# Decay factors from running sums of g by transposes and a DVE pass; the 16 columns for beta and steps ride on a chunk of v

## Chip, core and metric

One core of a Trainium2 chip runs the whole program; the metric is the device time of one execution in microseconds. PE is the matmul engine, DVE the vector engine, ACT the scalar engine, POOL the fourth compute engine, SP the engine that only issues transfers. Each engine takes its instructions in order and stops at the first one whose inputs, or whose output buffer, are not ready.

## The reference

Two blocks over 256 tokens of 1024 channels, all in fp32. The first block holds two attention layers and two feed-forward layers. The second, the "hybrid layer", projects the normed input by one wide matrix `w_in` and feeds two branches. The change touches the gated delta rule (8 heads) and the first head of the retention (4 heads):

```python
proj = xn @ w_in
qa, ka, va, za, beta_logit, a_dt, qb, kb, vb, gb, gate_a, gate_b = _split_cols(proj, IN_SIZES)
...
beta = jax.nn.sigmoid(beta_logit)
g = -jnp.exp(a_log) * jax.nn.softplus(a_dt + dt_bias)
oa = chunk_gated_delta_rule(qa, ka, va, beta, g)
...
g_cum = jnp.cumsum(g, axis=-1)
decay = jnp.exp(jnp.where(causal, g_cum[..., :, None] - g_cum[..., None, :], -jnp.inf))
...
lower = jnp.where(strict, jnp.einsum('bhncd,bhnmd->bhncm', k_beta, k) * decay, 0.0)
attn = jnp.where(causal, jnp.einsum('bhncd,bhnmd->bhncm', q, k) * decay, 0.0)
```

`beta_logit` and `a_dt` are 8 columns each of `w_in`, the 16 columns of the title; `vb` has 512 columns for each retention head. The kernel works with the delta rule over all 256 tokens as two tiles of 128, so a head's decay factors are three 128 x 128 blocks: tile 0 with itself, tile 1 with tile 0, tile 1 with itself.

## The kernel before

Every product with a weight is done as three: an fp32 operand is held as a high part and a low part, and hi x hi, hi x lo and lo x hi are summed in PSUM. Weights are streamed in pieces: a transfer brings `raw`, ACT writes the high part `hi` (line 188), DVE writes the low part `lo = raw - hi` (line 197, in passes of at most 512 columns), and PE multiplies (helper `mm`, line 134). One `hi`/`lo` half is 1024 columns; four halves and four `raw` buffers are in flight. Activations are split likewise: `OH`/`OL` hold the input of the second block before its norm's factors are known, `XH`/`XL` the normed one (`renorm`, lines 519 to 525). Transposes are fp32 matmuls against the identity (helper `tr`, line 145; it is also what turns a column of per-token factors into a row, as for `RT`).

A chunk is a run of products that ends in PSUM and has a post function that takes it out. The chunk kinds that matter here: `X_pair` (512 columns, tokens on the partitions, 8 pieces, two banks of 128x512), `X_chunk` (256 columns, 4 pieces, one bank), `N_chunk` (16 columns, columns on the partitions, 24 matmuls in one piece) and `W_pair` (two chunks of 256 columns at once, 8 pieces, two banks). Side work (norms, splits, attention, the decays) is written as Python generators; each call of `others()` after a piece runs every active generator to its next `yield`, and `pause(n)` lets n pieces pass. So the order of each engine's instructions is fixed when the program is built. PSUM has two banks of each of the tags `w` and a few of `s` and `d`; a tag's banks are taken in turn.

At the turn from the first block to the second the order is: the last feed-forward (`ffn(1, resid2)`); its residual `resid2`, which completes x by pairs of channel tiles, writes `REG` = x times a gain, splits it into `OH` and `OL` (ACT line 680, DVE line 691) and adds up the squares for two norms (`nacc` and `y`, lines 485 and 487); `X_pair(wvbp)`, which multiplies `OH`/`OL` by v of retention head 0, tile after tile as `resid2` delivers them, with the norms' sums over channels as small matmuls after its sixth piece; the factor `RT` by POOL (line 907) and its rows `RB`, `CR` (ACT lines 912 and 913); `N_chunk(wbda)` with the 16 columns; `W_pair(wqva)` for q, k and v of delta head 0; `W_chunk(wza)`, z of head 0; `wqka`, `wva` and so on for the next heads.

`decay_task` (line 937) starts from the 16 x 256 result of `N_chunk`: copied to SBUF, transposed to a token per partition, scaled by the norm's factor, then exp, log and a few passes over 16 columns make `BETA`, `NBETA` and `GG` (g, 8 heads by 2 tiles). For each head it spreads g over a 128 x 256 tile (two DVE passes, line 979), and six matmuls against constant triangles build sum differences and the mask in PSUM; ACT's Exp takes the 128 x 384 from PSUM to `DEC` (line 995). `DEC` lies in `REG`. The kernels of the delta rule (lines 1040 on) read it: `nLT` and `AT` at line 1076, with `DD` behind, line 1082.

Of the kernel before, what the change touches and what calls it, by code (L numbers as in the profile page):

```python
# [30 lines left out]
# steps that side work lets pass before it needs what others make for it  # L31
# [34 lines left out]
def body(ctx: ExitStack, tc: tile.TileContext, a):  # L66
# [17 lines left out]
    def PT(tag="side"):  # L84
        if tag == "side":
            # held within a step only: the bank taken longest ago
            age = {t: taken[t][-BANKS[t]] if len(taken[t]) >= BANKS[t] else 0 for t in "sd"}
            tag = "s" if side["dbusy"] or deferred or age["s"] <= age["d"] else "d"
        side["n"] += 1
        taken[tag].append(side["n"])  # L90
        return ps.tile([128, 512], F32, name="ps_" + tag, tag=tag, bufs=BANKS[tag])

# [16 lines left out]
    # the gains first, then x; what is needed later comes behind the first weights  # L109
# [45 lines left out]
    class Chunk:  # L155
        def __init__(self, src, cols, npieces, mm, pre=None, post=None):
# [3 lines left out]
            # pieces that come at once  # L160
# [47 lines left out]
    def ahead(i):  # L208
        """what may be loaded and split once the products of piece i are issued"""
# [50 lines left out]
    # tiles that are held over steps: no more of them than the ring has  # L260
# [17 lines left out]
    def wbank(more=0):  # L278
        """two banks in turn; two more while the norm's factors are on their way"""
        if len(deferred) >= 4:  # L280
            drain(cur["stat"])
            late(1)
        wn[0] += 1
        if len(deferred) + more >= 2 and wn[0] % 4 in (3, 0):
            return PT("d")
        return PT("w")

    wn = [0]
# [23 lines left out]
    def products(todo, xl_last=False):  # L312
        """(out, hi, lo, xh, xl, first, last): what was split last comes last"""
# [33 lines left out]
    def N_chunk(src, xs, n, post):  # L347
        """n < 128 columns in a piece"""
        def m(ck, s, hi, lo):
            xh, xl = xs  # L350
            ck.bank = PT("d")
            o = ck.bank[:n, :T]
            for k in range(8):
                c = slice(k * n, k * n + n)
                mm(o, hi[:, c], xh[:, k], k == 0, False)
                mm(o, hi[:, c], xl[:, k], False, False)
                mm(o, lo[:, c], xh[:, k], False, k == 7)
        return add(Chunk(src, 8 * n, 1, m, None, {0: lambda ck: wpost(post)(ck.bank)}))
# [4 lines left out]
    def D_chunk(grp, src, c, n, ops, post=None, pre=None, done=None):  # L363
        def m(ck, s, hi, lo):
            if c == 0:
                if s == 0:
                    grp.banks = [None] * 4
                    side["dbusy"] = True
# [21 lines left out]
    def D_tail(grp, src, n, ops, post, pre=None):  # L390
        """the last two chunks, a bank after the other"""
# [18 lines left out]
    def W_pair(src, xs, posts):  # L410
        """two chunks of outputs at once, over the tiles of x"""
# [23 lines left out]
    def X_pair(src, xs, posts):  # L435
        """512 columns, a bank for each half of the tokens"""
# [29 lines left out]
    def split(src, hi, lo):  # L466
        """the second part a step after the first"""
# [25 lines left out]
    def sum_ch(out, parts):  # L493
        """sums over the channels, a token per partition; 32 tokens at a time, as the weights' load is what they take"""
# [19 lines left out]
    def renorm():  # L514
        """the splits of x * g * r, for the chunks after the first"""
# [73 lines left out]
    # over the keys of two blocks, for the queries of the second: all of the first, or with the window  # L589
# [4 lines left out]
    # key > query: column > partition  # L594
# [16 lines left out]
    def attend(q, k, v, slot, window=False, sink=None, delay=0, done=False):  # L611
        """q, k: [128, T], a head on each half of the partitions; v(t, half) -> [128, 64]"""
# [38 lines left out]
        for h in range(2):  # L651
# [3 lines left out]
            # blocks: (q0, k0), (q1, k0), (q1, k1)  # L655
# [11 lines left out]
    # ================= the first block =================  # L667
# [7 lines left out]
    def feed_x(b, g, xs, norm, norm2=None, g2=None, first=False):  # L675
        """after xT's pair b is complete: x * g and its splits, the squares"""
# [31 lines left out]
    # attention of layer 0  # L708
# [59 lines left out]
    def tables():  # L768
        """of the second block"""
# [9 lines left out]
    # feed-forward with a short convolution  # L779
# [63 lines left out]
    # attention of layer 1  # L843
# [45 lines left out]
    # ================= between the blocks =================  # L889
# [7 lines left out]
    def stat2():  # L897
# [4 lines left out]
        # r1 = 1 / sqrt(mean x^2 + eps), and r1 r2 with r2 the factor of x g r1  # L902
# [23 lines left out]
    # ================= the second block =================  # L926
# [10 lines left out]
    def decay_task(bank):  # L937
        # beta and g, a token per partition
        b16 = TW([128, T], "e")
        cp("V", b16[:16], bank[:16, :T])  # L940
        yield
        p = PT("s")
        for t in range(2):
            PE.transpose(p[:, t * 16:t * 16 + 16], b16[:16, t * 128:t * 128 + 128], ident[:16, :16])
        bd = TW([128, 2, 16], "bd", 1)
        for t in range(2):
            V.tensor_scalar(bd[:, t], p[:, t * 16:t * 16 + 16], RTM[:, t:t + 1], None, op0=OP.mult)
# [3 lines left out]
        S.activation(e1, bd[:, :, 0:8], AF.Exp, scale=-1.0)  # L951
        S.activation(ea, P_("a_log"), AF.Exp)
        z = bd[:, :, 8:16]
# [20 lines left out]
        V.tensor_scalar(maskB, C_("gt"), -1e30, None, op0=OP.mult)  # L974

        def spread(h):
            gx = TW([128, 2, 128], "e")
            for t in range(2):
                V.tensor_scalar(gx[:, t], C_("le"), GG[:, t, h:h + 1], None, op0=OP.mult)
            return gx  # L980
        nx = spread(0)
        yield from pause(3)
        for h in range(8):
            gx = nx
            if h < 8 - 1:
                nx = spread(h + 1)
            yield
            p = PT()
            mm(p[:, 0:128], C_("gt"), gx[:, 0], True, False)
            mm(p[:, 0:128], identb, maskB, False, True)  # L990
            mm(p[:, 128:256], C_("gt"), GG[:, 0, h:h + 1].to_broadcast([128, 128]), True, False)
            mm(p[:, 128:256], ONES128, gx[:, 1], False, True)
            mm(p[:, 256:384], C_("gt"), gx[:, 1], True, False)
            mm(p[:, 256:384], identb, maskB, False, True)
            S.activation(DEC[:, h], p[:, :384], AF.Exp)
# [3 lines left out]
    def bda_post(bank):  # L999
        cur["dec"] = start(decay_task(bank))  # L1000

    def conv4(src, u, y, base):
        """src, u, y: [128, 2, T]; tiles base[i] of conv_a"""
# [37 lines left out]
    # the small blocks on the diagonal, and the transposes of the inverses  # L1041
# [4 lines left out]
    def delta_task(h, bank):  # L1046
# [6 lines left out]
        # the norms of k go into beta and v, those of q into the norm behind  # L1053
        tk, bk, nbk = (TW([128, 2], n, 1) for n in ("tk", "bk", "nbk"))
        qe, kv = (TW([128, 2], n, 3) for n in ("qe", "kv"))
        # the inverse, block by block of twice the size: D (0) and its transpose (1)
# [152 lines left out]
    def vb0_post(t):  # L1209
        def f(bank):  # L1210
            for c in range(2):
                if t == 0:
                    vbt[0, c] = hold([128, 2, 256], "v")
                cp("S", vbt[0, c][:, t], bank[:, c * 256:c * 256 + 256], RTM[:, t:t + 1])
        return f
# [554 lines left out]
```

## Time and profile before

| what | value |
|---|---|
| runs of the kernel | 1344.65, 1344.09, 1341.1 us |
| median | 1344.09 us |
| span of the profiled execution | 1341.2 us |
| that execution's own time | not recorded apart from its span; the median is 2.9 us above it |
| PE, DVE, ACT busy | 98%, 73%, 55% of the span |
| POOL busy | 2% |
| DMA | 215.79 MB, mean 161 GB/s |

The span is what the hardware profiler saw between the first and the last instruction of the one execution it recorded; the three runs are timed from outside. PE's share is that of matmuls whose ends are modelled. Times in the rows below are microseconds from the start of the span. In a row of the timeline the first number is the start, the second the duration of the group, `x4` the count of instructions in it, and `[0.31 <-DVE DD L1083]` an idle time before it with what ended it.

### The profile page before, as it was taken

Reading aid. Unit: us, or ns where it says so; the run is one execution under the profiler, and the core shown is the slowest. Engines: PE = TensorE matmul, PEld = TensorE weight load, DVE = VectorE, ACT = ScalarE, POOL = GpSimd, SP = SyncE. Lnnn points to the kernel's source line nnn. Section 1 sums busy time; section 2 is a strip of 40 time slices with the busy share of each in tenths; the row PEclk is TensorE's granted clock in tenths of the full one; section 3 lists DMA queues with packets and bytes.
Section 4 is the critical chain, followed back from the end, with each engine's and each line's share of the span. In section 5 each row is a group of like instructions: output and inputs, shape, how many; then the busy total and the mean of one; then the engine's idle time right before and its main releaser. Section 6 shows DMA issues by size and latency. Waiting matters only on the chain.

```text
span 1341.2 us, 29103 instructions
## 1 busy us (share of the span) xinstructions
PE 1317.4 (98%) x11824; PEld 1250.3 (93%) x11824; DVE 984.4 (73%) x2225; ACT 731.6 (55%) x1202; POOL 27.2 (2%) x38
## 2 busy tenths in 40 slices
PE   7999999999999999999999999999999999999998
PEld 6999999998889999999888888999999999999996
DVE  6997887778878877788778888666557556855554
ACT  6665765555765655566545544444343445655553
POOL 0000000000000000000000000000000000000000
PEclk9999999998999999999999999999999999999999
DMA  7435565554334655544333333445455564465652
GB/s 240 156 127 183 175 205 188 186 181 142 107 117 156 215 189 189 185 133 158 115 107 114 110 126 104 134 157 191 150 179 168 173 196 153 160 219 184 189 183 89
DMA packets 60470, 215.79 MB, mean 161 GB/s; under 512 B 6832, under 2 KB 7600, under 8 KB 60336
## 3 DMA queue, kind: packets, MB, share of 16 engines
q1 hardware_dynamic: 59328, 212.31, 49.1%
q8 instruction: 93, 1.52, 0.5%
q10 hardware_dynamic: 1008, 1.63, 0.4%
q14 instruction: 41, 0.34, 0.1%
HBM read 212.86 MB, written 1.05 MB: 159 GB/s over the span
## 4 chain that ended last, share of the span: by engine, by line
PE 92%; DVE 4%; ACT 2%; issue 1%; DMA 1%; POOL 0%; SPq 0%; POOLq 0%; DVEq 0%; ACTq 0%
PE ps_w L134 54%; PE ps_d L134 33%; PE ps_s L134 4%; PE ps_s L145 1%; ACT h L634 1%; DVE lo L197 1%; PE ps_d L145 1%; DMA xT<-in_x 0%; DMA raw<-in_wv0p 0%; DVE y L794 0%; ACT hi L188 0%; DVE XL L464 0%; DVE h L626 0%; DVE y L1369 0%; DVE DD L1082 0%
## 5 line engine op out<-in xcount | busy, mean ns | idle before, releaser
L197 DVE TENSOR_TENSOR lo<-raw,hi 128x512 fp32r<-128x512 f32 x801 | 519.7, 684 | 93.5 <-ACT hi L188 92.7
L188 ACT ACTIVATE hi<-raw 128x1024 fp32r<-128x1024 f32 (+1 forms) x403 | 418.1, 1046 | 168.9 <-PE ps_w L134 85.7
L134 PE MATMUL ps_w<-XH,hi 128*128 128x256 f32 x976 | 168.3, 295 | 2.5 <-ACT XH L1454 1.4
L134 PE MATMUL ps_w<-XL,hi 128*128 128x256 f32 x976 | 156.3, 283 | 0.0
L134 PE MATMUL ps_w<-XH,lo 128*128 128x256 f32 x976 | 156.1, 282 | 0.0
L134 PE MATMUL ps_w<-OH,hi 128*128 128x256 f32 x896 | 144.8, 284 | 0.0
L134 PE MATMUL ps_w<-OH,lo 128*128 128x256 f32 x896 | 142.9, 282 | 0.3 <-DVE lo L197 0.3
L134 PE MATMUL ps_w<-OL,hi 128*128 128x256 f32 x896 | 142.5, 281 | 0.0
L134 PEld LDWEIGHTS ps_w<-XH,hi 128*128 128x128 f32 x976 | 134.4, 191 | 7.8 <-ACT XH L1454 1.7
L134 PEld LDWEIGHTS ps_w<-XL,hi 128*128 128x128 f32 x976 | 133.8, 190 | 0.0
L134 PEld LDWEIGHTS ps_w<-XH,lo 128*128 128x128 f32 x976 | 133.6, 190 | 0.0
L134 PE MATMUL ps_d<-OH,hi 128*128 128x256 f32 x776 | 126.0, 283 | 0.0
L134 PEld LDWEIGHTS ps_w<-OH,hi 128*128 128x128 f32 x896 | 121.5, 188 | 3.6 <-issue 3.5
L134 PE MATMUL ps_d<-OL,hi 128*128 128x256 f32 x776 | 124.4, 281 | 0.0
L134 PE MATMUL ps_d<-OH,lo 128*128 128x256 f32 x776 | 124.3, 281 | 0.0
L134 PEld LDWEIGHTS ps_w<-OH,lo 128*128 128x128 f32 x896 | 122.1, 189 | 0.5 <-DVE lo L197 0.5
L134 PEld LDWEIGHTS ps_w<-OL,hi 128*128 128x128 f32 x896 | 121.7, 188 | 0.0
L134 PEld LDWEIGHTS ps_d<-OH,hi 128*128 128x128 f32 x776 | 104.9, 188 | 1.9 <-issue 1.7
L134 PEld LDWEIGHTS ps_d<-OL,hi 128*128 128x128 f32 x776 | 105.1, 187 | 0.3 <-DVE OL L470 0.2
L134 PEld LDWEIGHTS ps_d<-OH,lo 128*128 128x128 f32 x776 | 105.1, 188 | 0.2
L790 ACT ACTIVATE y<-u,prm 128x256 f32<-128x256 f32 x88 | 48.0, 595 | 62.4 <-DVE u L764 62.4
L764 DVE TENSOR_TENSOR u<-ps_w,RB 128x512 f32<-128x512 f32 x44 | 30.1, 689 | 63.0 <-PE ps_w L134 56.8
(378 smaller groups left out, 1644.7 us busy)
## 6 DMA issues: line engine op xcount, KB each, us to landing
raw<-in_wu SPq DMA_DIRECT2D x108, 512.0 KB, 4.2
raw<-in_wd SPq DMA_DIRECT2D x68, 512.0 KB, 3.9
raw<-in_wgb SPq DMA_DIRECT2D x24, 512.0 KB, 3.7
raw<-in_wqk SPq DMA_DIRECT2D x16, 512.0 KB, 4.0
raw<-in_wza SPq DMA_DIRECT2D x16, 512.0 KB, 3.8
raw<-in_wqkb SPq DMA_DIRECT2D x16, 512.0 KB, 4.1
raw<-in_wbra SPq DMA_DIRECT2D x16, 512.0 KB, 4.2
raw<-in_wbrb SPq DMA_DIRECT2D x16, 512.0 KB, 4.7
```

What stands on the lines that cost most here:

```text
L134: PE.matmul(out, lhsT, rhs, start=start, stop=stop, skip_group_check=True)
L145: PE.transpose(out, in_, ident)
L188: S.activation(hi[:, :w], raws[n][:, :w], AF.Copy)
L197: V.tensor_tensor(lo[:, c], raws[n][:, c], hi[:, c].bitcast(F32), op=OP.subtract)
L634: S.activation(e[h][:, c], e[h][:, c], AF.Exp, bias=nm[:, i:i + 1], accum_out=sums[:, i:i + 1])
L764: V.tensor_tensor(u, v2(bank), bc(RB, 2), op=OP.mult)
L790: S.activation(y[:, i], u[:, i], AF.Identity, bias=P_(cb, t), scale=P_(cw, 3 * t + 2))
```

## The change

The chunks at the turn are cut differently: `XN_chunk` multiplies 16 + 256 columns (the 16 for beta and the steps, and the first 256 of v of retention head 0) in one pass with tokens on the partitions, from four halves of 544 columns, and `X_chunk` does the other 256 columns; `X_pair` and `N_chunk` are gone. `vbd_post` scales the 16 columns from PSUM into `BD`, so that `decay_task` needs no copy and no transposes of its own, and starts it after tile 1. In `decay_task` three small matmuls make the running sums of g for all heads at once (`CUM`). For each head two transposes of a broadcast column of `CUM` put the sums along the free axis in PSUM; two DVE passes subtract the head's own column and take the minimum with a mask tile (0 or -1e30); ACT's Exp then works in place in `DEC`. `wbank` and `D_chunk` differ in when the sums' wait is drained and in which banks are taken. The comments of the file are gone as well; line numbers move by 4 and more.

```diff
-        if len(deferred) >= 4:
+        if len(deferred) + more >= 6:
             drain(cur["stat"])
-            late(1)
-        wn[0] += 1
-        if len(deferred) + more >= 2 and wn[0] % 4 in (3, 0):
-            return PT("d")
-        return PT("w")
-    wn = [0]
+            late()
+        return PT("w" if len(deferred) + more < 2 else "d")
...
-    def N_chunk(src, xs, n, post):
-        """n < 128 columns in a piece"""
+    def XN_chunk(src, xs, n, post):
+        w = 256 + n
         def m(ck, s, hi, lo):
             xh, xl = xs
-            ck.bank = PT("d")
-            o = ck.bank[:n, :T]
-            for k in range(8):
-                c = slice(k * n, k * n + n)
-                mm(o, hi[:, c], xh[:, k], k == 0, False)
-                mm(o, hi[:, c], xl[:, k], False, False)
-                mm(o, lo[:, c], xh[:, k], False, k == 7)
-        return add(Chunk(src, 8 * n, 1, m, None, {0: lambda ck: wpost(post)(ck.bank)}))
+            if s == 0:
+                ck.bank = [wbank(), wbank(1)]
+            todo = []
+            for kk in range(2):
+                k = 2 * s + kk
+                for t in range(2):
+                    tt = slice(t * 128, t * 128 + 128)
+                    c = slice(kk * w, kk * w + w)
+                    todo.append((ck.bank[t][:, :w], xh[:, k, tt], xl[:, k, tt], hi[:, c], lo[:, c], k == 0, k == 7))
+            products(todo, True)
+        ck = add(Chunk(src, 8 * w, 4, m, None, {3: lambda ck: [wpost(post(t))(ck.bank[t]) for t in range(2)]}))
+        ck.g = 1
...
+                    if deferred:
+                        drain(cur["stat"])
+                        late()
...
-    def decay_task(bank):
-        # beta and g, a token per partition
-        b16 = TW([128, T], "e")
-        cp("V", b16[:16], bank[:16, :T])
-        yield
-        p = PT("s")
-        for t in range(2):
-            PE.transpose(p[:, t * 16:t * 16 + 16], b16[:16, t * 128:t * 128 + 128], ident[:16, :16])
-        bd = TW([128, 2, 16], "bd", 1)
-        for t in range(2):
-            V.tensor_scalar(bd[:, t], p[:, t * 16:t * 16 + 16], RTM[:, t:t + 1], None, op0=OP.mult)
+    BD = T1([128, 2, 16], name="BD")
+    def decay_task():
+        yield from pause(1)
         e1, ea = TW([128, 2, 8], "e1", 1), TW([128, 8], "ea", 1)
         ax = TW([128, 2, 8], "axx", 1)
         sp = TW([128, 2, 8], "sp", 1)
-        S.activation(e1, bd[:, :, 0:8], AF.Exp, scale=-1.0)
+        S.activation(e1, BD[:, :, 0:8], AF.Exp, scale=-1.0)
         S.activation(ea, P_("a_log"), AF.Exp)
-        z = bd[:, :, 8:16]
+        z = BD[:, :, 8:16]
...
-        V.tensor_scalar(maskB, C_("gt"), -1e30, None, op0=OP.mult)
-        def spread(h):
-            gx = TW([128, 2, 128], "e")
-            for t in range(2):
-                V.tensor_scalar(gx[:, t], C_("le"), GG[:, t, h:h + 1], None, op0=OP.mult)
-            return gx
-        nx = spread(0)
-        yield from pause(3)
+        V.tensor_scalar(MW[:, 0:128], C_("gt"), -1e30, None, op0=OP.mult)
+        V.memset(MW[:, 128:256], 0.0)
+        yield from pause(2)
+        p = PT()
+        mm(p[:, 0:8], C_("le"), GG[:, 0], True, True)
+        mm(p[:, 8:16], C_("le"), GG[:, 1], True, False)
+        mm(p[:, 8:16], ONES128, GG[:, 0], False, True)
+        CUM = TW([128, 2, 8], "cum", 1)
+        V.tensor_copy(CUM.rearrange("p t h -> p (t h)"), p[:, 0:16])
+        yield from pause(1)
         for h in range(8):
-            gx = nx
-            if h < 8 - 1:
-                nx = spread(h + 1)
             yield
             p = PT()
-            mm(p[:, 0:128], C_("gt"), gx[:, 0], True, False)
-            mm(p[:, 0:128], identb, maskB, False, True)
-            mm(p[:, 128:256], C_("gt"), GG[:, 0, h:h + 1].to_broadcast([128, 128]), True, False)
-            mm(p[:, 128:256], ONES128, gx[:, 1], False, True)
-            mm(p[:, 256:384], C_("gt"), gx[:, 1], True, False)
-            mm(p[:, 256:384], identb, maskB, False, True)
-            S.activation(DEC[:, h], p[:, :384], AF.Exp)
+            for t in range(2):
+                tr(p[:, t * 128:t * 128 + 128], CUM[:, t, h:h + 1].to_broadcast([128, 128]))
+            V.scalar_tensor_tensor(DEC[:, h, 0:256], p[:, 0:256], CUM[:, 0, h:h + 1], MW, op0=OP.subtract, op1=OP.min)
+            V.scalar_tensor_tensor(DEC[:, h, 256:384], p[:, 128:256], CUM[:, 1, h:h + 1], maskB, op0=OP.subtract, op1=OP.min)
+            S.activation(DEC[:, h], DEC[:, h], AF.Exp)
...
-    def bda_post(bank):
-        cur["dec"] = start(decay_task(bank))
...
-    def vb0_post(t):
+    def vbd_post(t):
         def f(bank):
-            for c in range(2):
-                if t == 0:
-                    vbt[0, c] = hold([128, 2, 256], "v")
-                cp("S", vbt[0, c][:, t], bank[:, c * 256:c * 256 + 256], RTM[:, t:t + 1])
+            if t == 0:
+                vbt[0, 0] = hold([128, 2, 256], "v")
+            V.tensor_scalar(BD[:, t], bank[:, 0:16], RTM[:, t:t + 1], None, op0=OP.mult)
+            if t == 1:
+                cur["dec"] = start(decay_task())
+            cp("S", vbt[0, 0][:, t], bank[:, 16:272], RTM[:, t:t + 1])
         return f
+    def vb0_post(bank):
+        vbt[0, 1] = hold([128, 2, 256], "v")
+        for t in range(2):
+            cp("S", vbt[0, 1][:, t], bank[:, t * T:t * T + T], RTM[:, t:t + 1])
 
     for h in range(8):
         if h == 0:
-            X_pair(a["wvbp"], xsR, [vb0_post(t) for t in range(2)])
-            N_chunk(a["wbda"][0], xsR, 16, bda_post)
+            XN_chunk(a["wvbd"], xsR, 16, vbd_post)
+            X_chunk(a["wvb"][0], xsR, vb0_post)
             W_pair(a["wqva"], xsR, [qka_post(0), va_post(0)])
```

The order of the instructions at three places. First DVE where `resid2` takes out its last pair of channel tiles, whose `OL` the chunk of v waits for (before; `nacc`, `y` are the two norms' sums):

```order
L197 TENSOR_TENSOR lo<-raw,hi 128x512
L691 TENSOR_TENSOR OL<-REG,OH 128x512
L485 TENSOR_TENSOR nacc<-nacc,sq 128x512
L487 TENSOR_TENSOR nacc<-nacc 128x256
L485 TENSOR_TENSOR y<-y,sq 128x512
L487 TENSOR_TENSOR y<-y 128x256
L197 TENSOR_TENSOR lo<-raw,hi 128x512 x2
L691 TENSOR_TENSOR OL<-REG,OH 128x512
L197 TENSOR_TENSOR lo<-raw,hi 128x512
```

The same place now, with the lines moved by 4:

```order
L197 TENSOR_TENSOR lo<-raw,hi 128x512
L695 TENSOR_TENSOR OL<-REG,OH 128x512
L489 TENSOR_TENSOR nacc<-nacc,sq 128x512
L491 TENSOR_TENSOR nacc<-nacc 128x256
L489 TENSOR_TENSOR y<-y,sq 128x512
L491 TENSOR_TENSOR y<-y 128x256
L197 TENSOR_TENSOR lo<-raw,hi 128x32
L197 TENSOR_TENSOR lo<-raw,hi 128x512
L197 TENSOR_TENSOR lo<-raw,hi 128x32
L695 TENSOR_TENSOR OL<-REG,OH 128x512
L197 TENSOR_TENSOR lo<-raw,hi 128x512 x6
```

The weights' `lo` now comes in passes of 512 and 32 columns, and the last `OL` pass stands behind three of them. Its reader on PE was the seventh piece of eight of `X_pair`, behind the norms' sums; it is now the last of the four pieces of `XN_chunk`, ahead of them.

Second ACT, from the norm's rows `RB`, `CR` to the logarithm of the decays (`XH` is the renormed input; before):

```order
L912 COPY RB<-ps_s 128x256
L913 COPY CR<-ps_s 128x256
L138 ACTIVATE v<-ps_w,RT_97 128x256 x4
L525 ACTIVATE XH<-qn 128x512
L188 ACTIVATE hi<-raw 128x1024
L525 ACTIVATE XH<-qn 128x512
L188 ACTIVATE hi<-raw 128x1024
L525 ACTIVATE XH<-qn 128x512
L951 ACT_TABLE_LOAD
L951 ACTIVATE e_7960<-bd 128x16
L952 ACTIVATE ea<-prm 128x8
L956 ACTIVATE axx<-axx 128x16
```

And now:

```order
L916 COPY RB<-ps_s 128x256
L917 COPY CR<-ps_s 128x256
L138 ACTIVATE v<-ps_w,RT_97 128x256 x2
L138 ACTIVATE v<-ps_d,RT_97 128x256 x2
L529 ACTIVATE XH<-qn 128x512
L188 ACTIVATE hi<-raw 128x1024
L529 ACTIVATE XH<-qn 128x512
L949 ACT_TABLE_LOAD
L949 ACTIVATE e_7983<-BD 128x16
L950 ACTIVATE ea<-prm 128x8
L954 ACTIVATE axx<-axx 128x16
L529 ACTIVATE XH<-qn 128x512
```

The `v` passes come from two chunks, two from `ps_w` and two from `ps_d`, and are still behind `RB` and `CR`; the third `XH` pass stands between the exponentials and the second table load instead of ahead of the first.

Third PE, towards the end of `W_pair` (before; the six matmuls of head 0's decays are its last rows, those of `e`, `MW` and `GG`):

```order
L134 MATMUL ps_w<-OH,hi 128x256 x4
L134 MATMUL ps_w<-OL,hi 128x256 x4
L134 MATMUL ps_w<-OH,lo 128x256 x4
L134 MATMUL ps_w<-OH,hi 128x256 x4
L134 MATMUL ps_w<-OL,hi 128x256 x4
L134 MATMUL ps_w<-OH,lo 128x256 x4
L134 MATMUL ps_d<-e,cst 128x128
L134 LDWEIGHTS identb
L134 MATMUL ps_d<-MW,identb 128x128
L134 MATMUL ps_d<-GG,cst 128x128
L134 MATMUL ps_d<-e,ones 128x128
L134 MATMUL ps_d<-e,cst 128x128
```

And now, from the fifth piece of `W_pair` to the transposes of head 0:

```order
L134 MATMUL ps_w<-OH,hi 128x256 x4
L134 MATMUL ps_w<-OL,hi 128x256 x4
L134 MATMUL ps_w<-OH,lo 128x256 x4
L134 MATMUL ps_d<-GG,cst 128x8 x2
L134 MATMUL ps_d<-GG,ones 128x8
L134 MATMUL ps_w<-OH,hi 128x256 x4
L134 MATMUL ps_w<-OL,hi 128x256 x4
L134 MATMUL ps_w<-OH,lo 128x256 x4
L134 MATMUL ps_w<-OH,hi 128x256 x4
L134 MATMUL ps_w<-OL,hi 128x256 x4
L134 MATMUL ps_w<-OH,lo 128x256 x4
L145 MATMUL ps_d<-cst,cum 128x128 x2
```

The three 128x8 matmuls of the running sums are new and wait for `GG`; head 0's six matmuls have become two transposes of `cum`. Ahead of this stretch, `W_pair` now follows the row transposes at once, where the 24 matmuls of `N_chunk` stood between, and the two 128x16 transposes of line 944 behind its second piece are gone.

## Rows read from the trace of the kernel before

**Rows 1.** The page of before: engines; then the chain that ended last:

```profile
PE 1317.4 (98%) x11824; PEld 1250.3 (93%) x11824; DVE 984.4 (73%) x2225; ACT 731.6 (55%) x1202; POOL 27.2 (2%) x38
PE 92%; DVE 4%; ACT 2%; issue 1%; DMA 1%; POOL 0%; SPq 0%; POOLq 0%; DVEq 0%; ACTq 0%
```

**Rows 2.** The timeline of PE, from X_pair to W_pair (start, duration, what):

```profile
592.15 0.63 PE L134 MATMUL ps_w<-hi,OH 128*128 128x512 f32 x2
...
600.08 0.63 PE L134 MATMUL ps_w<-lo,OH 128*128 128x512 f32 x2
...
602.84 0.63 PE L134 MATMUL ps_w<-hi,OL 128*128 128x512 f32 x2
...
605.17 0.60 PE L145 MATMUL ps_s<-cst,RT 128*128 128x128 f32 x4
605.53 0.36 PE L134 MATMUL ps_d<-OH,hi 128*16 128x256 f32 x1
...
608.42 0.40 PE L134 MATMUL ps_w<-OH,hi 128*128 128x256 f32 x2
```

**Rows 3.** The timeline of PE, the decays, to the delta rule's DD:

```profile
611.36 0.29 PE L944 MATMUL ps_s<-cst,e 16*128 16x16 f32 x2
...
631.47 0.38 PE L134 MATMUL ps_d<-e,cst 128*128 128x128 f32 x2
...
634.72 0.72 PE L134 MATMUL ps_w<-XH,hi 128*128 128x256 f32 x4
...
645.92 0.35 PE L134 MATMUL ps_d<-DD,nLT 32*32 32x32 f32 x16 [0.31 <-DVE DD L1083]
```

**Rows 4.** The timeline of PE, a pair of fp32 128x128 transposes in retention:

```profile
702.15 0.38 PE L145 MATMUL ps_s<-cst,rt 128*128 128x128 f32 x2
702.37 0.60 PE L134 MATMUL ps_d<-AT,REG 128*128 128x256 f32 x2
```

**Rows 5.** The timeline of DVE, the end of resid2:

```profile
600.63 0.69 DVE L197 TENSOR_TENSOR lo<-raw,hi 128x512 fp32r<-128x512 f32 x1 [0.92 <-ACT hi L188]
601.24 0.68 DVE L691 TENSOR_TENSOR OL<-REG,OH 128x512 fp32r<-128x512 f32 x1
```

**Rows 6.** The timeline of ACT, the same stretch, to the passes of v:

```profile
599.55 2.19 ACT L188 ACTIVATE hi<-raw 128x1024 fp32r<-128x1024 f32 x3
...
605.81 0.37 ACT L912 COPY RB<-ps_s 128x256 f32<-128x256 f32 x1 [1.44 <-PE ps_s L145]
...
606.34 1.58 ACT L138 ACTIVATE v<-ps_w,RT 128x256 f32<-128x256 f32 x4
```

**Rows 7.** The timeline of ACT, then DVE: the chain to GG:

```profile
612.00 1.28 ACT L951 ACT_TABLE_LOAD   x1
613.30 0.22 ACT L951 ACTIVATE e<-bd 128x16 f32<-128x16 f32 x1
...
616.62 0.18 DVE L973 TENSOR_SCALAR GG<-sp 128x16 f32<-128x16 f32 x1
```

**Rows 8.** Groups of DVE instructions by line and shape:

```profile
L979 DVE TENSOR_SCALAR e<-cst,GG 128x128 f32<-128x128 f32 x16 | 3.8, 279 | 1.3 <-PE ps_s L134 1.3
L1076 DVE SCALAR_TENSOR_TENSOR nLT<-ps_d,nbk,REG 128x256 f32<-128x256 f32 x6 | 2.9, 478 | 0.0
```

**Rows 9.** The timeline of ACT, the tail of the decays and the first squares:

```profile
634.94 0.49 ACT L995 ACTIVATE REG<-ps_d 128x384 f32<-128x384 f32 x1 [0.62 <-PE ps_d L134]
...
641.88 0.42 ACT L1052 ACTIVATE sq<-qk 128x256 f32<-128x256 f32 x1
```

**Rows 10.** Timeline rows of PE behind two waits; two stretches, with PEclk, the granted clock:

```profile
325.27 0.43 PE L145 MATMUL ps_s<-cst,RTOK 128*128 128x128 f32 x2 [2.29 <-POOL RTOK L538]
326.00:333.00 7.00, 5.93 (x30) 5.67 (x29) 6.51 (x14) 2.02 (x3) 0.00 (x0) 0.53 0.42 134
1152.42 0.56 PE L134 MATMUL ps_w<-XH,hi 128*128 128x256 f32 x1 [1.42 <-ACT XH L1454]
1152.00:1157.00 5.00, 4.58 (x25) 4.58 (x26) 4.90 (x10) 2.05 (x4) 0.00 (x0) 0.66 0.00 0
```

More of the change, by code (lines that the diff above doesn't have):

```diff
@@ L1349, in body @@
         for c in range(2 if h else 0):
-            X_chunk(a["wvb"][2 * h + c - 2], xs0, vb_post(h, c))
+            X_chunk(a["wvb"][2 * h + c - 1], xs0, vb_post(h, c))
         if h > 0 and da[0] < 8:
@@ L1623, in wc @@
     def wc(w, cols):
-        return w[:, cols].reshape(8, 128, len(cols)).transpose(1, 0, 2).reshape(128, -1)
+        return np.ascontiguousarray(w[:, cols].reshape(8, 128, len(cols)).transpose(1, 0, 2).reshape(128, -1))
     def wset(w, collist):
@@ L1675, in pack @@
     gb2 = ga0 + 1024
-    out["wbda"] = wset(w, [b0 + r(16)])
+    out["wvbd"] = wc(w, np.concatenate([b0 + r(16), vb0 + r(256)]))
     qka = [np.concatenate([q0 + 128 * h + r(128), k0 + 128 * h + r(128)]) for h in range(8)]
@@ L1683, in pack @@
     out["wqkb"] = wset(w, [o + 256 * h + r(256) for h in range(4) for o in (qb0, kb0)])
-    out["wvbp"] = pair(w, vb0 + r(512))
-    out["wvb"] = wset(w, [vb0 + 256 * c + r(256) for c in range(2, 8)])
+    out["wvb"] = wset(w, [vb0 + 256 * c + r(256) for c in range(1, 8)])
     out["wgb"] = wset(w, [gb0 + 256 * c + r(256) for c in range(8)])
```

## The prediction

> **What bounds the kernel now.** I read the page first: PE is busy 98% of the span and 92% of the chain that ended last [rows 1], so time is won only where PE has less to do, and lost where PE is made to wait. PE's own timeline then shows a stretch, from X_pair to the first heads of the delta rule, with hardly an idle time in it [rows 2, 3]. So every microsecond of PE work that goes there counts, unless a wait that this work used to cover comes up. The timelines of DVE and ACT say where such covers are.
>
> Times are set against the profiled span of 1341.2 us. The median of the three runs is 1344.09, 2.9 more, and I add the change in the span to the median. About 0.3%, 4 us, is what a measurement of this kernel can tell from no change: under 1340.1 is faster, over 1348.1 slower.
>
> **PE work removed and added.** X_pair's matmuls of 512 columns start 0.233 us apart (34 of them between 592.15 and 600.08), so its 48 cost 11.2. The N_chunk's 24 take 605.53 to 608.42, 2.9, or 0.12 for 256 columns [rows 2]. Between these two, a matmul of 272 columns is 0.1275. Now 48 of 272 and 48 of 256 columns cost 6.1 + 5.8 = 11.9 against 14.1: **-2.2**. The sums over channels cost 1.8 (600.55 to 602.84, less a pair of 0.47) and stay.
>
> The two 16-row transposes go: **-0.3** by their row. Three heads of the decays took 631.47 to 634.72, so 1.08 for one and 8.7 for eight [rows 3]. Two transposes for a head take 0.22 in retention [rows 4], between other matmuls like here; with a little for breaking the stream I take 0.28, eight are 2.2. The lower end is 0.2, the upper the 1.08 of the old head, which would leave no gain. The three matmuls with 8 columns need weights of 128x128 each; nearest are the old fp32 matmuls of a head at about 0.2, so 0.7, between 0.1 and 1.1. Together 8.7 - 2.2 - 0.7: **-5.8**. PE work falls by 8.3 us in all.
>
> **Waits that come instead.** Five places.
>
> (1) *OL at the last piece of XN_chunk.* DVE writes the last OL from 601.24 on, behind a wait of 0.92 for ACT's hi [rows 5]; ACT's three hi passes there begin at 599.55, behind the squares of the norms [rows 6]. Before, PE read this OL at 602.84, after the sums [rows 2], and did not wait. Now it is read in the second product of XN_chunk's fourth piece, which PE would reach at 592.15 + 40 x 0.1275 = 597.3. The new hi passes are half as long and two lo passes shrink from 512 to 32 columns, so the OL pass ends at about 600.7 (600.1 if all of that helps, 601.9 if none). The eight matmuls that are left end at 601.7 and not at 598.3: **+3.4**. The norm's row transposes, at 605.17 before, come at 601.7 + 5.8 + 1.8 = about 609.3. I call this place R.
>
> (2) *Banks for W_pair.* It now follows the rows directly, and its two ps_w banks are held by XN_chunk until ACT has taken v out, behind RB and CR. The first v pass starts 1.17 after R [rows 2, 6], and two of them, half of the four's 1.58, end at about R + 1.9, where PE stands at R + 0.4. N_chunk's 2.9 us covered this: **+1.4**.
>
> (3) *GG for the running sums.* The sums stand behind W_pair's fifth piece: R + 1.9 + 60 x 0.12 = R + 9.1. GG was written at 616.62, R + 11.45 [rows 2, 7], by a chain that table loads of 1.28, DVE passes and its place behind renorm's passes make long. The transposes at its head go, but the log now stands behind one more XH, so I leave R + 11.3: **+2.3**. The ends are 0 (the chain moves up by the 0.6 us that the small transposes and their copy took, and by some queueing) and +3.3.
>
> A page differs here: the Trainium skill, "ScalarE: Activation LUTs", section "What ACT_TABLE_LOAD costs", counts 1.28 us for the load and about 1.38 for a drain, 2.66 in all. By it each load would hold the next activation another 1.4 us. The trace's load at 612.00 lasts 1.28, and the activation behind it started at 613.30, 0.02 after its end [rows 7], so the measurement decides and the sum stays.
>
> (4) *Bank and ACT at the end of the decays.* DVE has more to do for a head: a pass of 128x256 from PSUM is 0.48 and one of half the size at least the 0.28 of an old spread, together 0.76 or more against 0.56 for the two spreads [rows 8]. Heads 5 to 7 come in one place, and head 7 takes the bank of head 4, which DVE has to read first, behind passes of the convolution, about four heads' passes of 0.76 less the 1.4 in which PE does one piece: **+1.6**, between 0 and 3. Exp then ends late, and with it the passes that make q and k: **+0.5** at the first products of the delta rule.
>
> (5) *The first squares.* From the last head's Exp to the end of sq, which PE's next sums read, ACT's passes took 634.94 to 642.30, 7.4 [rows 9], and the change leaves them alone, while it makes PE's last three heads shorter by 0.8 each. So PE gets there early by up to 2.4, of which a part is already in (4): **+1.6**, between 0 and 2.4. The old wait of 0.31 for DD [rows 3] goes: **-0.3**.
>
> The sum: -8.3 + 3.4 + 1.4 + 2.3 + 1.6 + 0.5 + 1.6 - 0.3 = **+2.2**, and 1344.09 + 2.2 = **1346.3**; with the profile's own span, 1343.4. The saved matmuls are eaten up by chains on ACT and DVE that do not become shorter.
>
> **Rivals.**
>
> *B, PE's clock falls.* At 325.27 PE had waited 2.29 us, and the granted clock in 326 to 333 is 0.53 on average; at 1152.42 it had waited 1.42 and had 0.66 over 5 us, on its way to the lower of its two levels, 1.2 instead of 2.4 GHz, and back [rows 10]. So a fall costs 0.34 x 5 = 1.7 to 0.47 x 7 = 3.3 us. The wait for GG of 2.3 is as long as the one that fell, and is followed by three tiny matmuls; the stop at OL is the second candidate. This gives 1346.3 + 1.7 to 3.3 = 1348.0 to 1349.6, and with two falls of the larger price up to 1352.9: slower than before. It decides from a single wait of about 1.4 us on, the shorter of the two that fell. Against it: the waits may be split by pieces in between. The Trainium skill, "TensorE: Matmul & The Clock Gate", "Part 4: PE-mode transpose", says that transposes do not count as busy the same way; by that the places with six transposes in a row would be a third candidate, where 631.47 to 634.72 was full of matmuls before. No row here shows a fall at transposes: the pair at 702 is too short for it.
>
> *C, the chains follow PE.* If DVE and ACT are free enough to bring OL, v and GG sooner, the waits do not come, and PE's saving stands: 1344.09 - 8.3 = 1335.8; with (1) alone left 1339.2. For it speaks that DVE is busy only 73% and ACT 55% of the span [rows 1]; against it that OL is bound by data that resid2 delivers just then, and DVE ran from one pass to the next there.
>
> *D, the transposes cost as much as the old matmuls*, so that the change does not do what it is for on PE: PE's work falls by 2.2 + 0.3 - 0.7 = 1.8 only, and (1) to (3) stay, while (4) and (5) go because PE is later: -1.8 + 7.1 - 0.3 = +5.0, 1349.1. The pair at 702 speaks against it [rows 4], and I give it little.
>
> **Numbers.** My forecast, waits that eat the gain with no fall of the clock: 0.45, at 1346.3. B with D (0.31 and 0.05): 0.36, at 1348.0 to 1352.9. C and halves of it: 0.19, from 1335.8 to 1340. A part of the forecast's cases falls outside its band on either side in equal measure. So faster 0.19, same 0.45, slower 0.36. The range leaves out C in full and the two falls of B, and holds what the ends of the waits make of the forecast: 1337.5 to 1351.
>
> **What would show it.** In the profile after: PE's row of XN_chunk's fourth piece has a wait for DVE OL of 2 to 4 us, and the chunk ends near 601.7; the row transposes stand near 609.3, and W_pair's first matmul has a wait for ACT v of about 1.4; the 128x8 matmuls wait for DVE GG; two transposes of a head take under 0.3. DD of head 0 comes at about 648.1 where it was 645.92. PEclk under 1 between 600 and 626 would show B. If these rows have waits under 0.5 us and DD comes before 640, C holds and my forecast is wrong. If DD comes on time but the total moves, the cause lies elsewhere in the file, in banks of later chunks, and I have missed it.

## The result and the profile after

The changed kernel took 1361.13 us (median of 4 runs, 1358.97 to 1362.6), the kernel before 1343.87 beside it; the ratio is 1.013, 95% interval 1.0115 to 1.0145. The forecast was 1346.3 and the range ended at 1351: wrong, and on the slow side.

The timeline of PE of the changed kernel at the places that the prediction named (start, duration, what, wait before it):

```profile
597.78 0.67 PE L134 MATMUL ps_w<-hi,OH 128*128 128x272 f32 x4
...
604.01 0.52 PE L134 MATMUL ps_w<-lo,OH 128*128 128x272 f32 x2 [1.21 <-DVE lo L197]
605.00 0.77 PE L134 MATMUL ps_w<-hi,OH 128*128 128x272 f32 x4 [0.47 <-ACT hi L188]
606.43 1.13 PE L134 MATMUL ps_w<-hi,OL 128*128 128x272 f32 x4 [0.66 <-DVE OL L695]
...
616.56 0.60 PE L145 MATMUL ps_s<-cst,RT 128*128 128x128 f32 x4
618.27 0.87 PE L134 MATMUL ps_w<-OH,hi 128*128 128x256 f32 x4 [1.11 <-ACT v L138]
...
627.89 0.61 PE L134 MATMUL ps_d<-GG,cst 128*128 128x8 f32 x4 [2.04 <-DVE GG L971]
...
642.80 0.40 PE L145 MATMUL ps_d<-cst,cum 128*128 128x128 f32 x2 [2.40 <-DVE REG L991]
...
656.08 0.35 PE L134 MATMUL ps_d<-DD,nLT 32*32 32x32 f32 x16
```

All the waits are there. But XN_chunk, the first changed work, starts at 597.78, where X_pair started at 592.15 [rows 2]: 5.6 us were lost before any changed instruction. DD of head 0 comes 10.2 late (645.92 before [rows 3]), so the changed place adds 4.5, and the rest of the program, the same again, takes 1357.1 - 656.08 = 701.0 where it took 695.3: 5.7 more. 5.6 + 4.5 + 5.7 is the 15.9 by which the span grew.

So two thirds of the loss lie where nothing was changed. (The 5.6 and the 5.7 are not the pace alone: the granted clock also fell at other places, in before at the two of [rows 10], worth up to 3.3 and 1.7, and in the changed kernel in 15 to 20, where it was 0.66, worth up to 1.7.) PE's matmuls start further apart there. The timeline of PE of the changed kernel in the feed-forward layers of the first block, groups of four matmuls of 256 columns, three groups apart:

```profile
460.03 0.64 PE L134 MATMUL ps_d<-OL,hi 128*128 128x256 f32 x4
...
461.47 0.64 PE L134 MATMUL ps_d<-OL,hi 128*128 128x256 f32 x4
```

The same stretch of the kernel before:

```profile
460.09 0.63 PE L134 MATMUL ps_d<-OH,hi 128*128 128x256 f32 x4
...
461.51 0.64 PE L134 MATMUL ps_w<-OH,hi 128*128 128x256 f32 x4
```

Three groups take 1.44 us now and 1.42 before, 0.480 against 0.473 for one, with the granted clock at its full level in both. Some 7,850 matmuls of the program have a weight as the stationary operand and stand next to another of that kind; 1.6 ns more for each is 12.6 us. What the change does to them is not an instruction: `BD = T1(...)` is a new tile of 128 bytes per partition, allocated ahead of `raw`, `hi` and `lo`. By the memory map of the compiled programs, all hi and lo buffers start 160 bytes past a multiple of 256 before, and 32 past one after; XH, XL, OH and OL stay at 128. The sizes of the tiles in the source between OL and these buffers, each rounded up to 32 bytes, add up to the same distances: 32 past a multiple of 256 before, 160 after.

### The profile page after: what moved, and what is told of

Same layout as the page of the kernel before. It is cut to its first block, busy times and chain, and to the rows that moved or that the text cites. A ratio compares the mean times of both kernels' runs of the same rounds, so it can differ in the third digit from the quotient of the medians.

```text
span 1357.1 us, 29039 instructions
## 1 busy us (share of the span) xinstructions
PE 1322.5 (97%) x11788; PEld 1256.8 (93%) x11788; DVE 987.0 (73%) x2229; ACT 731.9 (54%) x1203; POOL 27.6 (2%) x38
## 4 chain that ended last, share of the span: by engine, by line
PE 89%; DVE 6%; ACT 3%; issue 1%; DMA 0%; POOL 0%; SPq 0%; POOLq 0%; DVEq 0%; ACTq 0%
PE ps_w L134 51%; PE ps_d L134 32%; PE ps_s L134 4%; DVE lo L197 1%; PE ps_s L145 1%; PE ps_d L145 1%; ACT hi L188 1%; ACT h L638 1%; DMA xT<-in_x 0%; DVE h L630 0%; DVE OL L695 0%; DVE y L798 0%; DVE REG L142 0%; DVE XL L468 0%; DVE nacc L489 0%
## 5 line engine op out<-in xcount | busy, mean ns | idle before, releaser
L188 ACT ACTIVATE hi<-raw 128x1024 fp32r<-128x1024 f32 (+2 forms) x404 | 418.2, 1044 | 174.5 <-PE ps_w L134 82.9
```

Of the source, the lines that this page charges most:

```text
L188: S.activation(hi[:, :w], raws[n][:, :w], AF.Copy)
```

## The experiments

**The place of the buffers by itself.** Theory L: the place sets the pace. Rival S: the pace belongs to the changed instructions, or to the chip. First the place without the change:

```diff
     GG = T1([128, 2, 8], name="GG")
+    T1([128, 32], name="PAD")
```

> The kernel before with an unused tile of 128 bytes per partition where the change puts BD, so that the weights' raw, hi and lo buffers, and all that lies behind, move by 128 bytes as they do in the changed kernel; no instruction differs. Theory L (the place of the weights' buffers sets the matmuls' pace): groups of four 256-column matmuls start 0.48 us apart instead of 0.473, and the time is 1344 + about 11 to 13 = 1355 to 1357. Rival S (the slower pace belongs to the changed instructions, or to the chip that ran them): the pace stays 0.473 and the time 1344.

Measured: 1356.03, ratio 1.0097 (1.008 to 1.0115) to the kernel before. The timeline of PE, four groups apart:

```profile
459.78 0.64 PE L134 MATMUL ps_w<-OH,lo 128*128 128x256 f32 x4
...
461.71 0.64 PE L134 MATMUL ps_d<-OH,hi 128*128 128x256 f32 x4
```

1.93 for four, 0.48 each. L holds: an unused tile costs 12.8 us. Then the change without the place:

```diff
-    BD = T1([128, 2, 16], name="BD")
...
             if t == 0:
+                bdt["x"] = TW([128, 2, 16], "bd", 1)
```

> The changed kernel with BD taken from the working pool when it is first written, behind the weights' buffers, so that raw, hi and lo lie where they lay before. Theory L: pace 0.473 again and a time of about 1361 - 12 = 1349, which is the 4 us that the waits and clock falls at the changed place cost. Rival S: 1361.

Measured: 1350.09, ratio 1.0054 (1.0035 to 1.0073). The place is worth 11 us of the 17.3. The change's own work costs 6.7 against 1343.4, the kernel before over all its runs, and 6.9 against the 1343.24 measured beside this run. The timeline of PE of this run:

```profile
592.50 0.66 PE L134 MATMUL ps_w<-hi,OH 128*128 128x272 f32 x4
...
612.00 0.60 PE L145 MATMUL ps_s<-cst,RT 128*128 128x128 f32 x4
...
623.33 1.02 PE L134 MATMUL ps_d<-GG,cst 128*128 128x8 f32 x4 [2.13 <-DVE GG L972]
...
641.28 0.40 PE L145 MATMUL ps_d<-cst,cum 128*128 128x128 f32 x2 [2.46 <-DVE REG L992]
...
654.55 0.35 PE L134 MATMUL ps_d<-DD,nLT 32*32 32x32 f32 x16
```

XN_chunk starts at 592.50, 0.35 from before's X_pair, and the rest behind DD takes 1349.5 - 654.55 = 695.0, as before. So all that is lost, is lost between them: 8.3 us. Its windows (span of the window, busy times of PE, PEld, DVE, ACT, POOL, then the granted clock, DMA share and GB/s):

```profile
595.00:605.00 10.00, 7.80 (x39) 6.83 (x38) 8.46 (x16) 6.77 (x10) 0.00 (x0) 0.72 0.56 179
605.00:610.00 5.00, 5.00 (x120) 4.85 (x119) 0.76 (x4) 1.06 (x2) 0.30 (x1) 0.87 0.80 263
...
620.00:630.00 10.00, 7.87 (x42) 7.67 (x41) 5.13 (x19) 5.31 (x6) 0.00 (x0) 0.67 0.33 107
...
640.00:650.00 10.00, 8.26 (x66) 8.04 (x67) 9.32 (x22) 7.64 (x12) 0.00 (x0) 1.00 0.41 129
```

The clock fell behind the stops at OL and lo, and again behind the wait for GG: 0.28 x 10 + 0.13 x 5 + 0.33 x 10 = up to 6.8 us of the 8.3. That is rival B, twice.

**Which places are fast.** Four places at once:

```diff
-        hi = TW([128, 1024], "hi", LA + 1, F32R)
+        hi = TW([128, 1032], "hi", LA + 1, F32R)
...
-            parts[n].append(TW([128, 1024], "lo", LA + 1, F32R))
+            parts[n].append(TW([128, 1032], "lo", LA + 1, F32R))
```

> The kernel before with each hi and lo buffer 32 bytes longer, so that the four hi buffers start at 160, 192, 224 and 0 and the four lo buffers at 32, 64, 96 and 128 bytes past a multiple of 256 (before: all at 160; changed: all at 32). Theory L: the pace of the matmuls differs from one hi buffer to the next in turn, with lo at 32 the slow one (0.120 each) and hi at 160 the old one (0.1183); whether another place is faster still is what the run is to show. Rival S: one pace for all.

Measured: 1336.0 (one run). The timeline of PE shows the buffers in turn, each for six groups, the first rows of three of them:

```profile
202.46 0.64 PE L134 MATMUL ps_w<-OH,hi 128*128 128x256 f32 x4
202.94 0.65 PE L134 MATMUL ps_w<-OL,hi 128*128 128x256 f32 x4
...
205.33 0.63 PE L134 MATMUL ps_w<-OH,hi 128*128 128x256 f32 x4
205.80 0.64 PE L134 MATMUL ps_w<-OL,hi 128*128 128x256 f32 x4
...
208.15 0.62 PE L134 MATMUL ps_w<-OH,hi 128*128 128x256 f32 x4
208.60 0.62 PE L134 MATMUL ps_w<-OL,hi 128*128 128x256 f32 x4
```

0.48, 0.47 and 0.45 for a group, by the buffer. Sorted by the stationary operand's buffer over the whole run, hi at 192 had 114.5 ns from start to start and lo at 64 had 113.9; hi at 160 had 118.1, the others 117.0 to 119.7. The 117.0 is that of lo at 32, the place that has 119.9 when all buffers lie there, so the pace of one load also depends on what runs beside it. A control:

```diff
+    T1([128, 64], name="PAD")
```

> The kernel before with an unused tile of 256 bytes at the same place. If L holds and what counts is the place within 256 bytes: 1344 and pace 0.473. If any move of these buffers against OH and XH slows the matmuls: slower, as with 128 bytes. Rival S: 1344.

Measured: 1343.92 (one run): a move by 256 changes nothing. Then all buffers at 192:

```diff
     GG = T1([128, 2, 8], name="GG")
+    T1([128, 8], name="PAD")
```

> The kernel before with an unused tile of 32 bytes, so that all hi and lo buffers start 192 bytes past a multiple of 256, the place that in the run with four places had the fastest matmuls (114.5 ns against 118.3). No instruction differs. If the place sets the pace: 7,850 matmuls with a weight as the stationary operand gain 4 ns each, 31 us, so about 1313, less where DVE or ACT (73% and 55% busy) then hold PE up. If the fast place in that run was due to the buffers lying at different places, and not to this one: 1344.

Measured: **1313.0**, ratio 0.9772 (0.9757 to 0.9786), as forecast. This beats both kernels by a tile that nobody reads. The changed kernel with hi and lo at 64:

```diff
     GG = T1([128, 2, 8], name="GG")
+    T1([128, 8], name="PAD")
...
     BD = T1([128, 2, 16], name="BD")
```

> The changed kernel with 32 more unused bytes behind BD, so that hi and lo start at 64 bytes past a multiple of 256 (changed: 32). By the place theory with 64 as good as 192: 1361 - 7,850 x 6 ns = about 1314, and the difference to the kernel before at its own fast place is what the change itself costs, about 4 to 7. If only 192 is fast: 1355 or more.

Measured: 1339.14, ratio 0.9968 (0.9955 to 0.9981), neither 1314 nor 1355: with all buffers at 64 the mean is 117.2 ns. It is a mean of two paces. Two stretches of PE's timeline in this run, rows three groups apart:

```profile
460.18 0.63 PE L134 MATMUL ps_w<-OH,hi 128*128 128x256 f32 x4
...
461.59 0.63 PE L134 MATMUL ps_w<-OH,hi 128*128 128x256 f32 x4
...
1030.36 0.62 PE L134 MATMUL ps_d<-OH,hi 128*128 128x256 f32 x4
...
1031.73 0.62 PE L134 MATMUL ps_d<-OH,hi 128*128 128x256 f32 x4
```

1.41 and 1.37, with a full clock in both: most of the run went at 117.8 ns, some hundreds of matmuls at 113.3. So 64 is a place that allows the fast pace too, and mostly did not get it in this run. Last, whether the place counts against the activations' place:

```diff
+    T1([128, 8], name="PAD")
     xT = T1([128, 8, T], name="xT")
```

> The kernel before with 32 unused bytes ahead of all large tiles: hi and lo at 192 as in the run with 32 bytes behind GG, but the activations XH, XL, OH and OL move along, from 128 to 160. If the weights' own place counts: 1313 and 114 ns. If the place of the weights against that of the activations counts: 1344 and 118.3 ns as before.

Measured: 1340.22 (one run), not 1313. The timeline of PE:

```profile
460.09 0.64 PE L135 MATMUL ps_w<-OH,lo 128*128 128x256 f32 x4
...
461.51 0.64 PE L135 MATMUL ps_w<-OH,lo 128*128 128x256 f32 x4
```

Three groups in 1.42, the pace of before, though hi and lo lie at 192: of the weights' place and their distance to the activations, the distance is what counts. In one table, with times of the runs and the mean time from start to start of successive matmuls of 256 columns that load hi or lo, from the trace:

| run | hi, lo | XH to OL | distance, within 256 | ns per matmul | us |
|---|---|---|---|---|---|
| before | 160 | 128 | 32 | 118.3 | 1343.4 |
| moved by 256 | 160 | 128 | 32 | 118.3 | 1343.9 |
| changed, BD in the working pool | 160 | 128 | 32 | 118.3 | 1350.1 |
| all moved by 32 | 192 | 160 | 32 | 118.3 | 1340.2 |
| changed | 32 | 128 | 160 | 119.9 | 1361.1 |
| before, moved by 128 | 32 | 128 | 160 | 119.9 | 1356.0 |
| changed, 32 more | 64 | 128 | 192 | 117.2 (two paces) | 1339.1 |
| before, moved by 32 | 192 | 128 | 64 | 114.5 (two paces) | 1313.0 |

At 32 and at 160 both kernels have the same pace, whatever their instructions.

**The parts of the change, at the old place.** The decays alone:

```diff
-            mm(p[:, 0:128], C_("gt"), gx[:, 0], True, False)
...
+            for t in range(2):
+                tr(p[:, t * 128:t * 128 + 128], CUM[:, t, h:h + 1].to_broadcast([128, 128]))
```

> The kernel before with the decay part of the change alone (running sums, transposes, a DVE pass, Exp in place), the sums one piece later than in the change; X_pair, N_chunk and the place of the weights' buffers stay as before. My sum's terms: PE work -5.8, no wait for GG, the wait for head 7's bank and those at q, k and the first squares stay, together about +4: 1344 - 2 = 1342, +1.7 for each fall of the clock. The rival that the decay part is what costs: 1346 or more.

Measured: 1339.85, ratio 0.997 (0.9959 to 0.9982): a gain of 3.6. Waits of PE by releaser (us in total, times, longest):

```profile
PE ps_d L145 <- DVE REG L989: 1.8, 1, 1.8
...
PE ps_d L134 <- ACT sq L1047: 1.4, 1, 1.4
...
PE ps_s L134 <- ACT qk L1017: 0.5, 1, 0.5
```

GG is not among them; the sums stand a piece later and N_chunk's 2.9 us still lie ahead. The chunks alone:

```diff
-            X_pair(a["wvbp"], xsR, [vb0_post(t) for t in range(2)])
-            N_chunk(a["wbda"][0], xsR, 16, bda_post)
+            XN_chunk(a["wvbd"], xsR, 16, vbd_post)
+            X_chunk(a["wvb"][0], xsR, vb0_post)
```

> The chunk part of the change alone (XN_chunk and X_chunk instead of X_pair and N_chunk, BD straight from PSUM), with the decays as before and the weights at the old place. My terms: PE work -2.5, the waits at OL and lo +2.2 and at the banks of v +1.1, no wait for GG, since the old spreads stand two pieces later: 1344 + 1, and +3.3 if the clock falls at OL as it did in the full change: 1344 to 1348. The rival that the chunk part is harmless and the decays cost: under 1342.

Measured: 1348.43, ratio 1.0042 (1.0025 to 1.0059), just above the upper end. The same view:

```profile
PE ps_w L134 <- DVE lo L197: 1.5, 2, 1.2
...
PE ps_w L134 <- ACT v L138: 1.1, 1, 1.1
...
PE ps_w L134 <- DVE OL L695: 0.6, 2, 0.4
```

The chunk part costs 5.0 and the decay part gains 3.6. Together they cost 6.7 instead of 1.4. What the traces show beyond the parts is the wait for GG, 2.13, and more of the clock's falls: two worth up to 6.8 in the run shown, against one of 0.17 x 10 = 1.7 with the chunks alone (0.83 in 600 to 610). The last wait of the decays, by other banks for heads 6 and 7:

```diff
-            p = PT()
+            p = PT("s" if h > 5 else "side")
```

> The decay part alone at the old place, with heads 6 and 7 given the other two banks, so that PE need not wait for DVE at head 7 (1.76 us in the run of the decay part). If PE's wait there is what costs: 1339.9 - 1.8 = 1338. If DVE's passes and the Exp behind them set the end of the decays anyway, the wait only moves to the products of q and k and to the squares: 1339.9, the same.

Measured: 1340.35, ratio 0.9976 (0.9967 to 0.9986), the same as without it. The same view:

```profile
PE ps_d L134 <- ACT qk L1017: 1.7, 1, 1.7
...
PE ps_d L134 <- ACT sq L1047: 1.4, 1, 1.4
...
PE ps_s L145 <- DVE REG L989: 0.5, 1, 0.5
```

The wait of 1.76 has become 0.5, and that for q and k 1.7 where it was 0.5. DVE's passes and the Exp behind them set the end there, and a free bank only moves the wait.

**Both kinds of gain together.** The changed kernel and the decay part, each at the fast place (the tile of 32 bytes above):

> The changed kernel with BD in the working pool and 32 unused bytes, so that the weights lie at 192 as in the run of the kernel before that took 1313.0. If the change's own cost is that of its waits and clock falls, it is the same here as at the old place (1350.1 - 1343.4 = 6.7, of which up to two falls of 3.3 come and go): 1313 + 1 to 8, so 1314 to 1321. If the new tiles cost something else through their places: more.

Measured: 1326.69, ratio 0.9882 (0.9868 to 0.9897): 13.7 above the kernel before at that place, more than expected. By the trace the matmuls took 115.5 ns on average and not 114.5, for the reason that the next run shows; 7,850 x 1.0 is 7.9 us, and the 5.8 that are left lie within the expected 1 to 8.

> The decay part alone with the weights at the fast place. The two gains should add, as they are on different work: 1313.0 - 3.6 = 1309.4, which would beat both kernels. If PE is by now held up by ACT and DVE at the decays, part of the 3.6 goes: 1311 to 1313.

Measured: 1316.83 (1312.49 to 1319.02), ratio 0.9803 (0.9783 to 0.9822), 3.8 slower than the kernel before at that place instead of 3.6 faster. The two intervals just touch (0.9757 to 0.9786 there), so that it is slower is not certain; that the gains do not add is. The timelines of PE of the two show why, in a stretch where both have the same instructions with the same buffers. The kernel before at the fast place, three groups apart:

```profile
460.13 0.62 PE L134 MATMUL ps_d<-OL,hi 128*128 128x256 f32 x4
...
461.49 0.62 PE L134 MATMUL ps_d<-OL,hi 128*128 128x256 f32 x4
```

The decay part at the fast place:

```profile
460.32 0.64 PE L134 MATMUL ps_w<-OL,hi 128*128 128x256 f32 x4
...
461.74 0.64 PE L134 MATMUL ps_w<-OL,hi 128*128 128x256 f32 x4
```

1.36 against 1.42: this place too allows the two paces, 113.3 and 117.8 ns for a matmul, each held over hundreds of matmuls. Over some 1,250 matmuls in the feed-forward layers the decay part ran at the slower one and the kernel before at the faster, some 5.6 us (1,250 x 4.5 ns). The same two passes of ACT ahead of and behind this stretch confirm it; first the kernel before at the fast place:

```profile
427.43 1.05 ACT L188 ACTIVATE hi<-raw 128x1024 fp32r<-128x1024 f32 x1
...
576.72 1.04 ACT L188 ACTIVATE hi<-raw 128x1024 fp32r<-128x1024 f32 x1
```

The decay part:

```profile
430.31 1.04 ACT L188 ACTIVATE hi<-raw 128x1024 fp32r<-128x1024 f32 x1
...
585.31 1.04 ACT L188 ACTIVATE hi<-raw 128x1024 fp32r<-128x1024 f32 x1
```

It was 2.9 behind ahead of the stretch and 8.6 behind it, 5.7 more; that stretch alone turns the expected gain of 3.6 around. The changed kernel ran at the slower pace there too. What sets which pace is taken was not found, and so the 3.6 us of the decay part are shown at the old place only.

## Why the prediction was wrong

**The step that failed** is the one in which I set the sum against the span and added the difference to the median: it takes for granted that the rest of the program runs as before. I priced every instruction that `BD` is written and read by, and gave the tile itself no term. It measured +11 to +12.8 us. My own last test, "If DD comes on time but the total moves, the cause lies elsewhere in the file", was near the right question, but it did not fit what came (DD was 10.2 late, 5.6 of it from ahead of the change), and I looked for the cause in banks.

With the buffers back at their old place the time, 1350.1, lies inside the range. That is no success of the forecast's path: its sum had no fall of the clock, and this run had two.

**The changed place, by the run with the buffers at their old place** (changed kernel in brackets where it differs):

| term | forecast | measured |
|---|---|---|
| waits at lo, hi, OL (1) | +3.4 | 2.2 (2.7) |
| banks of v (2) | +1.4 (by its own figures 1.5) | 1.1 |
| GG (3) | +2.3 (by its own figures 2.2) | 2.1 (2.0) |
| bank of head 7; q and k (4) | +1.6; +0.5 | 2.5 (2.4); 0.5 (none) |
| first squares (5) | +1.6 | 1.4 (0.6) |
| old wait for DD | -0.3 | -0.3 |
| clock | 0 (rival B: 1.7 to 3.3 a fall) | +6.8 (3.4) |

DD came 8.3 late, 1.5 if the falls cost their full 6.8; the forecast was 2.2. So the waits and the saved PE work were right within a microsecond in sum, with a smaller wait at OL and a larger one at head 7.

**Rival B**, with 0.31 and two falls priced at up to 6.6, is what the changed place did; I had it as less likely than no fall. Its point of decision, "a single wait of about 1.4 us on", does not hold as a rule. The windows of the changed kernel:

```profile
600.00:610.00 10.00, 7.34 (x41) 6.46 (x40) 8.66 (x17) 6.57 (x10) 0.00 (x0) 0.83 0.56 187
620.00:630.00 10.00, 7.96 (x67) 7.75 (x66) 7.04 (x26) 8.20 (x12) 0.00 (x0) 1.00 0.18 63
640.00:650.00 10.00, 7.60 (x52) 7.39 (x51) 9.56 (x24) 6.28 (x10) 0.00 (x0) 0.83 0.34 108
```

Here the clock stayed up behind the 2.04 for GG and fell behind the 2.40 at head 7; with the buffers at the old place it was the other way round, behind 2.13 and 2.46. The falls cost 1.7 (0.17 x 10) to 3.4 each, near the price taken from [rows 10]; which wait they follow can't be told from its length. Even the first wait of [rows 10] shows it. In the run with all places moved by 32, with the instructions of the kernel before, the timeline and a window:

```profile
325.31 0.43 PE L146 MATMUL ps_s<-cst,RTOK 128*128 128x128 f32 x2 [2.28 <-POOL RTOK L539]
326.00:333.00 7.00, 5.75 (x49) 5.57 (x49) 6.71 (x14) 3.12 (x4) 0.00 (x0) 1.00 0.43 133
```

The same wait, 2.28, is followed by a clock of 1.00 where before had 0.53.

The rule that transposes do not count as busy the same way (the Trainium skill, "TensorE: Matmul & The Clock Gate", "Part 4: PE-mode transpose") is not decided here. At the six transposes of heads 5 to 7 the clock fell in the changed kernel (0.83 above), but with the same transposes and the longer wait in the run with the buffers at their old place the window from 640 to 650 has a clock of 1.00. No run here puts transposes without a wait to the test.

The table loads took 1.28 and no more, as the prediction held against the 2.66 of the Trainium skill ("ScalarE: Activation LUTs", "What ACT_TABLE_LOAD costs"). The timeline of ACT of the changed kernel:

```profile
621.30 1.28 ACT L949 ACT_TABLE_LOAD   x1
622.59 0.22 ACT L949 ACTIVATE e<-BD 128x16 f32<-128x16 f32 x1
```

**Rival C** (no waits) is out: all five places have theirs. **Rival D** (transposes as dear as matmuls) is out: with the running sums alone the kernel gains 3.6, and in the changed kernel head 0's two transposes start at 631.54 and the matmuls behind them at 631.68, 0.14 later.

## What to carry to other kernels

A new tile is part of a change: look where it puts the buffers behind it, and compare the pace of the same matmuls in a stretch that the change does not touch before reading anything else. An unused tile of the same size in the old kernel is the control, and trying a few sizes can be worth more than the change: 32 bytes gave 2.3% here. A size that is good in one version is to be measured again in the next, since the same place can take either of two paces. When a saving on PE uncovers chains on other engines, price the clock's falls with the waits, since they were most of what this one cost at its own place.

## What the hardware showed unexpectedly

The pace of matmuls that load a weight each time depended on the distance between the stationary and the moving operand's buffers, within 256 bytes: 118.3 ns at 32, 119.9 at 160, and 113.3 or 117.8 at 64 and at 192. The times of 1313.0 and 1339.1 at these two are therefore also a matter of how much of the run goes at which pace, and not of the place alone. The distances 96, 128, 224 and 0 were seen only in the run with four places, beside others (118.1 to 119.7 by the buffer); whether it is these two reads that meet was not tried. The two paces are both seen in one run, with the granted clock full in both stretches; at 64 two runs have different paces at the same instructions. The changed kernel and its version with the buffers at the old place have waits of nearly the same length at the same instructions, and differ in where the granted clock falls.
